# RMSNorm with ReLU: half of VectorE's loop replaced by whole-chunk instructions, with shared reciprocals and the last store split in two

## Chip, cores, metric

One core of one Trainium2 chip. The metric is the device time of one execution in microseconds (us); all times below are of runs with a granted clock of 1.0 in each. The "span" of a profile is some 1.3 us shorter than the time of the same run (158.9 against 160.25 for the profiled run of the kernel before). Times of single DMA packets ("packet records") are given here on the same clock as the instructions of the profile. The recorded prediction and expectations read them from an origin some 0.035 us earlier, so their packet times are that much too high against their issue times (the first packet of the kernel before starts at 1.755 us, and the prediction has 1.79).

## The reference

```python
def reference(x, gamma, eps):          # x: (16, 1024, 512) float32, gamma: ones(512), eps 1e-5
    rms = np.sqrt(np.mean(x ** 2, axis=-1, keepdims=True) + eps)
    x_norm = x / rms * gamma
    return np.maximum(x_norm, 0).astype(np.float32)
```

16,384 rows of 512 floats: 33.55 MB come in and 33.55 MB go out.

## The kernel before

Each of the 128 partitions takes 128 rows, as eight chunks of 16 rows (4 MB over all partitions). The kernel keeps six chunks on chip, so chunks 6 and 7 reuse the places of chunks 0 and 1, once those have been stored. SyncE (SP) issues every large transfer on one queue, in this order: the loads of chunks 0 to 5 (chunk 0 in two halves), the stores of chunks 0 and 1, the loads of chunks 6 and 7, a store of chunks 2 and 3 together (rows 32 to 63, "the middle store" below), a store of chunks 4 and 5, and the stores of chunks 6 and 7. ScalarE squares and sums the rows and takes the roots, 8 rows a pass. VectorE scales, multiplies by gamma and cuts at 0.

```python
    # SP: the order of the transfers, and what each waits for
    order = [(L, 0, G), (L, G, G)] + [(L, i * K, K) for i in range(1, nslots)] + [
        (S, 0, K), (S, K, K), (L, room, K), (L, room + K, K),
        (S, 2 * K, 2 * K), (S, 4 * K, 2 * K), (S, room, K), (S, room + K, K)]
    ...
        if kind == S:
            if order[m - 1][0] == L:                       # the first store after a load
                nc.sync.wait_ge(tick, 6 if a == 0 else 11)
            nc.sync.wait_ge(done, (a + r) // G)
        elif a >= room:
            take(nc.sync, sems[order.index((S, a - room, r))], 16)
        transfer(m)
    ...
    # VectorE: 12 passes of 8 rows for chunks 0 to 5 ...
    ndyn = nslots * per
    with nc.vector.Fori(0, ndyn) as gi:
        ...
        nc.vector.wait_ge(sq, 1)                            # ScalarE's root of this pass
        nc.vector.reciprocal(...)                           # 8 columns
        for j in range(G):                                  # 8 times 512 elements
            r = nc.vector.scalar_tensor_tensor(out=row, in0=row, scalar=rstd[...],
                in1=gamma_sb, op0=ALU.mult, op1=ALU.mult)
            if j == G - 3:
                r.then_inc(tick, 1)
        ...
        nc.vector.tensor_scalar_max(out=blk, in0=blk, scalar1=0.0).then_inc(done, 1)
    # ... and chunks 6 and 7 whole
    for i in range(nslots, nchunks):
        nc.vector.wait_ge(sq, per * (i - nslots + 1))
        nc.vector.reciprocal(...)                           # 16 columns
        nc.vector.tensor_tensor(out=blk, in0=blk, in1=fac[:, :, None].to_broadcast([P, K, d]), op=ALU.mult)
        nc.vector._custom_dve(dve_ops.TENSOR_MUL_SAT, out=blk, in0=blk,      # times gamma, cut at 0
            in1=gamma_sb[:, None, :].to_broadcast([P, K, d]), s0=float("inf"), s1=0.0).then_inc(done, per)
```

## Time and profile before

| | before |
|---|---|
| time, median of 6 runs | 160.28 us (160.15 to 160.50) |
| span of the profiled run | 158.9 us |
| moved by the large queue | 67.11 MB, 98.3% of the 16 DMA engines' span |
| VectorE busy | 129.4 us (81%), last instruction ends at 145.5 |
| ScalarE busy | 86.3 us (54%), last root near 114 |

The groups of instructions of the page, with busy us and mean ns of one, and after the second bar the idle time in front of them:

```profile
L153 DVE SCALAR_TENSOR_TENSOR slots<-slots,rstd,gamma_sb 128x512 f32 x96 | 64.7, 746 | 1.8 <-DVE rstd L148 1.8
L160 DVE TENSOR_SCALAR slots<-slots x12 | 27.5, 2294 | 0.4
L173 DVE CUSTOM_DVE_ANT_1 slots<-slots,gamma_sb 128x8192 f32<-128x8192 f32 x2 | 17.4, 8693 | 0.3
L170 DVE TENSOR_TENSOR slots<-slots,rstd 128x8192 f32<-128x8192 f32 x2 | 17.4, 8692 | 0.1
```

### The profile page before, as it was taken

The page shows a single profiled execution, that of the slowest core. Times are in us where ns is not written, and L with a number is a line of the kernel's source. Part 1 is how long each engine was busy: PE and PEld are TensorE (multiplying, and loading weights), DVE is VectorE, ACT ScalarE, POOL GpSimd, SP SyncE. Part 2 cuts the span into 40 slices and gives each one's busy share as a digit, 9 for nine tenths or more (in the row PEclk, how much of TensorE's full clock was granted, in tenths as well). Part 3 has the DMA queues.
Part 4 walks back from the last instruction along what each step waited for, and adds up shares of the span by engine and source line. Part 5 has one row for each costly group of instructions (what it writes and reads, how often), then busy time and mean ns, then how long its engine had stood idle before and what let it go on. Part 6 is the DMA issues. An engine that isn't in the chain of part 4 may idle for free.

```text
span 158.9 us, 902 instructions
## 1 busy us (share of the span) xinstructions
DVE 129.4 (81%) x128; ACT 86.3 (54%) x273; POOL 0.8 (0%) x6
## 2 busy tenths in 40 slices
DVE  0013999999999999999999999999999999996000
ACT  0388919889889989988930098898600000000000
POOL 1000000000000000000000000000000000000000
DMA  6999999999999999999999999996997998999996
GB/s 194 406 454 449 470 404 396 495 429 396 429 487 404 396 462 462 396 404 495 421 396 404 503 412 396 528 495 297 528 478 313 528 412 379 396 396 503 412 404 264
DMA packets 2168, 67.12 MB, mean 422 GB/s; under 512 B 244, under 2 KB 244, under 8 KB 248
## 3 DMA queue, kind: packets, MB, share of 16 engines
q1 hardware_dynamic: 2160, 67.11, 98.3%
q10 hardware_dynamic: 8, 0.01, 0.0%
HBM read 33.56 MB, written 33.55 MB: 422 GB/s over the span
## 4 chain that ended last, share of the span: by engine, by line
DVE 51%; issue 18%; DVEq 5%; ACT 3%; ACTq 0%; POOLq 0%
DVE slots L153 27%; DVE slots L170 11%; DVE slots L173 11%; DVEq L153 3%; ACT junk L130 3%; DVE rstd L148 1%; DVEq L143 1%; DVEq L148 0%; ACTq L130 0%; DVE rstd L168 0%; DVE slots L160 0%; ACT rms L135 0%; DVEq L162 0%; DVEq L172 0%; ACTq L135 0%
## 5 line engine op out<-in xcount | busy, mean ns | idle before, releaser
L130 ACT ACTIVATE junk<-slots 128x512 f32 x128 | 74.4, 581 | 21.9 <-POOLq L117 17.4
L153 DVE SCALAR_TENSOR_TENSOR slots<-slots,rstd,gamma_sb 128x512 f32 x96 | 64.7, 746 | 1.8 <-DVE rstd L148 1.8
L160 DVE TENSOR_SCALAR slots<-slots x12 | 27.5, 2294 | 0.4
L130 ACT ACTIVATION_READ_ACCUMULATOR junk<-slots x128 | 23.9, 186 | 0.0
L173 DVE CUSTOM_DVE_ANT_1 slots<-slots,gamma_sb 128x8192 f32<-128x8192 f32 x2 | 17.4, 8693 | 0.3
L170 DVE TENSOR_TENSOR slots<-slots,rstd 128x8192 f32<-128x8192 f32 x2 | 17.4, 8692 | 0.1
L148 DVE RECIPROCAL rstd<-rms x12 | 2.3, 195 | 5.4 <-ACT rms L135 5.4
L141 DVE LOAD_MASK_SELECT gamma_sb<-gseed x1 | 0.0, 14 | 8.0 <-DMA gseed<-in_gamma_dram 8.0
L135 ACT ACTIVATE rms<-ss,eps_sb x16 | 4.8, 301 | 1.8
L123 ACT ACT_TABLE_LOAD x1 | 1.3, 1283 | 4.0 <-issue 4.0
L141 DVE STREAM_SHUFFLE gamma_sb<-gseed 128x512 f32<-128x512 f32 x1 | 0.7, 717 | 0.0
L112 POOL MEMSET gseed<- 128x512 f32 x1 | 0.5, 525 | 1.9 <-POOLq L97 1.9
L168 DVE RECIPROCAL rstd<-rms 128x16 f32<-128x16 f32 x2 | 0.5, 246 | 0.0
L203 POOL MEMSET const-bfloat16-1.0<- 128x1 bf16 x1 | 0.1, 101 | 0.0
L203 POOL MEMSET const-uint8-127<- 128x1 uint8 x1 | 0.1, 101 | 0.0
L203 POOL MEMSET const-float32-0.0<- 128x1 f32 x1 | 0.1, 98 | 0.2 <-issue 0.2
L203 POOL MEMSET const-float32-1.0<- 128x1 f32 x1 | 0.1, 98 | 0.0
L113 POOL MEMSET eps_sb<- 128x1 f32 x1 | 0.1, 98 | 0.0
## 6 DMA issues: line engine op xcount, KB each, us to landing
slots<-in_x_dram SPq DMA_DIRECT2D x7, 4096.0 KB, 29.8
out_dram<-slots SPq DMA_DIRECT2D x4, 4096.0 KB, 17.4
slots<-in_x_dram SPq DMA_DIRECT2D x2, 2048.0 KB, 9.7
out_dram<-slots SPq DMA_DIRECT2D x2, 25.6
gseed<-in_gamma_dram ACTq DMA_DIRECT2D x1, 8.0 KB
```

Source lines behind the costliest of these rows:

```text
L112: nc.gpsimd.memset(gseed, 0.0).then_inc(sem_z, 1)
L123: nc.scalar.preload_act_table(ACTF.Sqrt)
L130: a = nc.scalar.activation(out=junk[:, j, :], in_=slots[:, bass.ds(base + j * d, d)], func=ACTF.Square, accum_out=ss[:, bass.ds(col + j, 1)])
L135: nc.scalar.activation(out=rms[:, bass.ds(col, G)], in_=ss[:, bass.ds(col, G)], func=ACTF.Sqrt, bias=eps_sb, scale=inv_d).then_inc(sq, 1)
L141: nc.vector.stream_shuffle(gamma_sb, gseed, [0] * 32)
L143: with nc.vector.Fori(0, ndyn) as gi:
L148: nc.vector.reciprocal(out=rstd[:, bass.ds(col, G)], in_=rms[:, bass.ds(col, G)]).then_inc(sv, 1)
L153: r = nc.vector.scalar_tensor_tensor(out=row, in0=row, scalar=rstd[:, bass.ds(col + j, 1)], in1=gamma_sb, op0=ALU.mult, op1=ALU.mult)
L160: nc.vector.tensor_scalar_max(out=blk, in0=blk, scalar1=0.0).then_inc(done, 1)
L168: nc.vector.reciprocal(out=fac, in_=rms[:, i * K:(i + 1) * K]).then_inc(sv, 1)
L170: nc.vector.tensor_tensor(out=blk, in0=blk, in1=fac[:, :, None].to_broadcast([P, K, d]), op=ALU.mult).then_inc(sv, 1)
L173: nc.vector._custom_dve(dve_ops.TENSOR_MUL_SAT, out=blk, in0=blk, in1=gamma_sb[:, None, :].to_broadcast([P, K, d]), s0=float("inf"), s1=0. ...
```

## The change

The intent: VectorE issues fewer, larger instructions. It loops over chunks 0 to 2 only and takes chunks 3 to 7 whole; chunks 4 and 5 share one reciprocal, and so do chunks 6 and 7. The middle store is held until 10 groups of 8 rows are done (it waited for the eleventh pass's tick), and the last chunk's second multiply and its store are cut into two halves of 8 rows.

```diff
+    looped = 3
...
-        (S, 2 * K, 2 * K), (S, 4 * K, 2 * K), (S, room, K), (S, room + K, K)]
+        (S, 2 * K, 2 * K), (S, 4 * K, 2 * K), (S, room, K),
+        (S, room + K, G), (S, room + K + G, G)]
...
-                nc.sync.wait_ge(tick, 6 if a == 0 else 11)
+                nc.sync.wait_ge(*((tick, 6) if a == 0 else (done, 10)))
...
-    ndyn = nslots * per
+    ndyn = looped * per
...                                  (the loop over chunks 6 and 7 is replaced by)
+    for first, last in ((3, 3), (4, 5), (6, 7)):
+        nc.vector.wait_ge(sq, per * (last + 1 - looped))
+        whole(nc.vector.reciprocal, out=rstd[:, first * K:(last + 1) * K],
+              in_=rms[:, first * K:(last + 1) * K])
+        nc.vector.wait_ge(sv, steps)
+        for i in range(first, last + 1):
+            blk = here(i * K, K)
+            whole(nc.vector.tensor_tensor, out=blk, in0=blk,
+                  in1=rstd[:, i * K:(i + 1) * K, None].to_broadcast([P, K, d]), op=ALU.mult)
+            nc.vector.wait_ge(sv, steps)
+            r = G if i == nchunks - 1 else K
+            for a in range(i * K, (i + 1) * K, r):
+                blk = here(a, r)
+                nc.vector._custom_dve(dve_ops.TENSOR_MUL_SAT, out=blk, in0=blk,
+                    in1=gamma_sb[:, None, :].to_broadcast([P, r, d]),
+                    s0=float("inf"), s1=0.0).then_inc(done, r // G)
```

`whole` emits an instruction, increments the semaphore `sv` on its end and counts.

## The prediction

> **What bounds the kernel now.** I read the page's summary first, to ask which resource is never idle.
>
> ```profile
> span 158.9 us, 902 instructions
> DVE 129.4 (81%) x128; ACT 86.3 (54%) x273; POOL 0.8 (0%) x6
> DMA  6999999999999999999999999996997998999996
> q1 hardware_dynamic: 2160, 67.11, 98.3%
> HBM read 33.56 MB, written 33.55 MB: 422 GB/s over the span
> ```
>
> VectorE (DVE) is busy 81% of the span and is the largest part of the "chain that ended last", which invites the reading "VectorE bounds it". But the one queue that carries x in and the result out occupies the 16 DMA engines for 98.3% of the span. The dips in the DMA row are a binning effect: in the records of single DMA packets, cut across slices of 2 us, the share is 1.00 in every slice from 2.5 us to the last one. A 32,768 B packet takes 1213 ns, a 65,536 B one 2419 and a 16,384 B one 611, so 27.0 GB/s per engine whatever the piece, 432 GB/s together. 67.11 MB at 432 GB/s is 155.3 us. Add 1.79 us before the first packet and about 0.5 us from the last packet to the last signal, and some 1.3 us is left of 158.9: the ramp of the first packets, and the lag of the slowest engine, whose last packet ends at 158.46 while the others end between 157.63 and 158.13. So this is a DMA-bound kernel with a full pipe, and the question for any VectorE change is only whether a transfer is ever issued too late.
>
> For that I read the timeline of the issuing engine (SP) and of VectorE.
>
> ```profile
> 58.55 0.82 SPq L82 DMA_DIRECT2D out_dram<-slots  x2
> 71.38 10.26 SPq L82 DMA_DIRECT2D slots<-in_x_dram  x2
> 98.45 0.34 SPq L82 DMA_DIRECT2D out_dram<-slots  x1
> 110.08 0.34 SPq L82 DMA_DIRECT2D out_dram<-slots  x1
> 127.81 0.33 SPq L82 DMA_DIRECT2D out_dram<-slots  x1
> 145.53 0.33 SPq L82 DMA_DIRECT2D out_dram<-slots  x1
> ```
>
> Columns: start, duration, place. Against these the packet records give the times at which the transfers in front leave the engines: the store of rows 32 to 63, issued at 98.45, sends its first packets at 99.54 to 100.13, engine by engine[...]. The store issued at 110.08 waits in the queue until about 119, the one of 127.81 until 138.3, and the last, of 145.53, starts at 147.96 to 148.77. All wait behind another transfer; the slack of the 98.45 store is by far the smallest.
>
> [...]the first load is issued at 0.73 us, its first packets start on the 16 engines at 1.79 to 2.24. I use the measured 1.06 to 1.51 us. [...]the 4096-element tensor_scalar of L160 takes 2294 ns, the 8192-element tensor_tensor of L170 8692. [...]
>
> **The change part by part.**
>
> ```profile
> 59.88 2.29 DVE L160 TENSOR_SCALAR slots<-slots  x1
> 62.09 0.19 DVE L148 RECIPROCAL rstd<-rms  x1
> 80.48 0.30 ACT L135 ACTIVATE rms<-ss,eps_sb  x1
> 109.97 0.25 DVE L168 RECIPROCAL rstd<-rms 128x16 f32<-128x16 f32 x1
> 110.25 8.69 DVE L170 TENSOR_TENSOR slots<-slots,rstd 128x8192 f32<-128x8192 f32 x1
> 119.09 8.69 DVE L173 CUSTOM_DVE_ANT_1 slots<-slots,gamma_sb 128x8192 f32<-128x8192 f32 x1
> 127.70 0.25 DVE L168 RECIPROCAL rstd<-rms 128x16 f32<-128x16 f32 x1
> ```
>
> *Removed:* six of twelve loop passes. A pass starts every 7.98 us, so 16 rows cost 15.96 us. *Added:* three chunks of 16 rows taken whole. Start to start a whole chunk is 127.70 - 109.97 = 17.73 us: 0.28 for the reciprocal, 8.84 for the multiply with its wait, 8.61 for the custom one. So whole chunks are dearer, 1.77 us each, since they lose the double-rate maximum. Over the whole, VectorE's instruction count falls but its work grows.
>
> Walking VectorE's new order, with those intervals: the loop's sixth pass ends as now, and chunk 3 starts at 62.09. Its custom instruction starts at 62.09 + 0.28 + 8.84 = 71.21, and the next instruction could start at 79.82. That is the shared reciprocal of chunks 4 and 5, which needs ScalarE's twelfth root: 80.48 + 0.30 = 80.78, and 0.16 us to release VectorE (first one: root ends at 14.05, reciprocal starts at 14.21), so 80.94. This is a **new wait of 1.1 us**. A 32-column reciprocal I put at 0.35 us (8 columns 195 ns, 16 columns 246, so 6.4 ns a column). Multiply at 81.33, custom at 90.17, its end at 98.86.
>
> There `done` reaches 10, which the store of rows 32 to 63 now waits for: issue at 98.86 + 0.03 = **98.89 in place of 98.45**. Going on: chunk 5's multiply 98.78, custom 107.62 to 116.31, store of rows 64 to 95 issued 116.34 (now 110.08; needed by about 119). Shared reciprocal of chunks 6 and 7 at 116.23; ScalarE ends its sixteenth root near 114, so no wait. Multiply 116.62, custom 125.46 to 134.15, store of chunk 6 issued 134.18 (now 127.81; needed at 138.3 less 1.5). Chunk 7: multiply 134.07, first half 142.91 to 147.34, store issued **147.37**; second half 147.26 to 151.69, store issued **151.72**. VectorE thus ends 6.2 us later than its 145.5 of now.
>
> What that does to the DMA. Middle store: descriptors ready at 98.89 + 1.06 to 1.51, which is 99.95 to 100.40, on engines that become free at 99.54 to 100.13. The engines idle 0.3 to 0.4 us on average, for the first time. But the end is set by the slowest engine, free at 100.13: it loses 0 to 0.27, say 0.15, plus something for a first packet after idleness (the first load's first packets took 719 to 1502 ns against 611; behind a store I put 0.15 to 0.3). First half-store: ready at 148.43 to 148.88, against engines free at 147.96 to 148.77 plus about 0.35 of delay: some engines lose 0.1 more. Second half-store: ready at 152.78 to 153.23, its predecessor runs 8 x 0.611 = 4.89 us from 148.4 on, so until at least 153.2: no loss. Packets of 16 KB: 16 x 611 = 9.78 us against 8 x 1.213 = 9.70, so 0.07. Sum: 0.15 + 0.2 + 0.05 + 0.07, about 0.45 us later.
>
> The split of the last store is what pays for VectorE's lateness. Unsplit, the last store would be issued at about 151.6 (134.07 + 8.84 + 8.69), ready at 152.7 or later, and need 9.7 us more: past 162.4, or some 4 us too late.
>
> The metric's run is 160.31 where the span is 158.9 (a constant near 1.4). So 160.31 + 0.45 = **160.75 us**.
>
> **The rivals.** (a) *The DMA queue hides everything:* [...]only the 0.07 of smaller packets is seen: 160.3 to 160.4. For it: the store is now issued 1.09 us ahead of its first packet[...]. Against it: those 1.09 are just the shortest latency that the first load shows, so there may be no slack left. (b) *VectorE becomes the bound at the end:* if each whole chunk costs 0.3 us more than the two seen, or the shared reciprocals wait longer, then the last halves are issued 1.5 us later and the last store starts late on idle engines: 151.72 + 1.5 + 1.5 + 4.9 + 0.5 = 160.1 of span, 161.5 of time. For it: no run shows a whole chunk beside loads and a busy ScalarE throughout. Against: chunk 6 ran beside ScalarE till 114 and took the same 8.69 as chunk 7. (c) *VectorE was the bound and fewer instructions help:* the chain of waits speaks for it, since it runs along VectorE to 145.5. The packet records refute it, as the last store waits another 2.4 us for the engines; and whole chunks cost more, not less. I give it no time below 160.
>
> **Range and chances.** Rival (a) gives the low edge, 160.2 with the runs' scatter of 0.1; the sum with all its terms at their larger values (0.27 + 0.5 + 0.2 + 0.07) gives 161.3, and (b) 161.5. Range 160.2 to 161.4. Faster by 2% would mean 157.1, less than the DMA work plus its ends allow: 0.01. Slower by 2%, 163.5, needs VectorE's last half 3 us behind my sum: 0.02. Within 2%: 0.97.
>
> **What would show each step right or wrong.** Two reciprocals of 32 columns, the first waiting about 1.1 us for ScalarE; five pairs of 8.69 us[...]; VectorE ending near 151.7; stores issued at 98.9, 116.3, 134.2, 147.4 and 151.7; in the packet records a first gap on the engines near 100 us, and perhaps one near 148.4, and none elsewhere. A DMA share of 1.00 through 100 us makes (a) right. An idle pipe between the last two stores makes (b) right. The prediction is wrong if the packets' own durations change, which nothing here would explain.

The sum came to 0.45 us over 160.31, so 160.75. What the traces change for the reader:

- The 432 GB/s are measured (32,768 B in 1213 ns on each of 16 engines, in the profiles before and after alike). That no faster rate is to be had is not shown; the prediction takes the measured rate as given.
- The 4.43 us of each half in VectorE's walk: half of the whole one's 8692 ns would be 4.35 us, which puts the last two issues 0.08 and 0.17 us earlier. The 0.05 us for the first half-store are reckoned with the 4.43. 4.42 us was measured.
- "Descriptors ready", and in late8's expectation "reach an idle engine", stands for the issue plus a measured delay to the first packet: here that of the first load (1.06 to 1.51 us on 15 engines, 1.91 on the last, on the prediction's clock). The profile shows issues and packets only.
- In the packet records of the kernel before, the middle store's first packet follows the end of the engine's last load by 2 to 3 ns on 15 engines, and one engine is idle for 0.12 us, from 99.70.
- The "double-rate maximum" is, in the trace, the loop's tensor_scalar: 2294 ns for 4096 elements, 0.56 ns an element, against 1.06 for the custom multiply (8693 ns for 8192).

## The result

Ratios in this document are the mean time of one kernel's fast runs over that of the other's of the same rounds, so they are not quite the ratio of the medians quoted.

| | before | after |
|---|---|---|
| time, median | 160.28 us (6 runs, 160.15 to 160.50) | 160.11 us (6 runs, 159.92 to 160.22) |
| ratio | | 0.9986, 95% interval 0.9973 to 0.9999 |
| VectorE's last instruction ends | 145.5 us | 151.1 us |

Within 2%, as expected, but on the other side of 160.28 from the predicted 160.75, and under the range's low edge of 160.2. The summary of the page after:

```profile
span 158.6 us, 770 instructions
DVE 135.2 (85%) x76; ACT 86.3 (54%) x273; POOL 0.8 (0%) x6
DMA  6999999999999999999999999997969969999997
q1 hardware_dynamic: 2304, 67.11, 98.6%
```

VectorE is busy 5.8 us longer with 52 fewer instructions, and the large queue still fills the DMA engines. VectorE's timeline after (start, duration, idle time in front in brackets) and the timeline of SP's issues:

```profile
59.70 2.29 DVE L161 TENSOR_SCALAR slots<-slots  x1
61.91 0.24 DVE L168 RECIPROCAL rstd<-rms 128x16 f32<-128x16 f32 x1
71.03 8.69 DVE L185 CUSTOM_DVE_ANT_1 slots<-slots,gamma_sb 128x8192 f32<-128x8192 f32 x1
80.61 0.35 DVE L168 RECIPROCAL rstd<-rms 128x32 f32<-128x32 f32 x1 [0.89 <-ACT rms L136]
89.82 8.69 DVE L185 CUSTOM_DVE_ANT_1 slots<-slots,gamma_sb 128x8192 f32<-128x8192 f32 x1
...
142.38 8.76 DVE L185 CUSTOM_DVE_ANT_1 slots<-slots,gamma_sb 128x4096 f32<-128x4096 f32 x2
```

```profile
98.54 0.34 SPq L83 DMA_DIRECT2D out_dram<-slots  x1
115.96 0.34 SPq L83 DMA_DIRECT2D out_dram<-slots  x1
133.78 0.33 SPq L83 DMA_DIRECT2D out_dram<-slots  x1
146.84 4.67 SPq L83 DMA_DIRECT2D out_dram<-slots  x2
```

The reader should see that the order is as worked out, down to the new wait of 0.89 us for ScalarE, but all of it 0.2 to 0.6 us ahead of the worked-out times. In the packet records of this profile one engine out of 16 pauses at 99.51 us, for 0.09 us; apart from such pauses near 7 us, where gamma comes in, there is no other of that length.

### The profile page after: what moved, and what is told of

Read it like the earlier page. It is cut to its first block, busy times and chain, and to the rows that moved or that the text cites. A ratio compares the mean times of both kernels' runs of the same rounds, so it can differ in the third digit from the quotient of the medians.

```text
span 158.6 us, 770 instructions
## 1 busy us (share of the span) xinstructions
DVE 135.2 (85%) x76; ACT 86.3 (54%) x273; POOL 0.8 (0%) x6
## 3 DMA queue, kind: packets, MB, share of 16 engines
q1 hardware_dynamic: 2304, 67.11, 98.6%
## 4 chain that ended last, share of the span: by engine, by line
DVE 44%; ACT 27%; issue 6%; ACTq 4%; DVEq 0%; POOLq 0%
ACT junk L131 26%; DVE slots L185 22%; DVE slots L168 22%; ACTq L131 3%; ACTq L126 1%; DVE rstd L168 0%; ACT rms L136 0%; ACTq L136 0%; ACTq L139 0%; DVEq L181 0%; POOLq L118 0%
## 5 line engine op out<-in xcount | busy, mean ns | idle before, releaser
L185 DVE CUSTOM_DVE_ANT_1 slots<-slots,gamma_sb 128x8192 f32<-128x8192 f32 (+1 forms) x6 | 43.5, 7269 | 0.6
L168 DVE TENSOR_TENSOR slots<-slots,rstd 128x8192 f32<-128x8192 f32 x5 | 43.4, 8689 | 0.1
L154 DVE SCALAR_TENSOR_TENSOR slots<-slots,rstd,gamma_sb 128x512 f32 x48 | 32.3, 747 | 0.9 <-DVE rstd L149 0.9
L161 DVE TENSOR_SCALAR slots<-slots x6 | 13.8, 2294 | 0.2
L149 DVE RECIPROCAL rstd<-rms x6 | 1.2, 196 | 5.1 <-ACT rms L136 5.1
L168 DVE RECIPROCAL rstd<-rms 128x32 f32<-128x32 f32 (+1 forms) x3 | 0.9, 315 | 0.9 <-ACT rms L136 0.9
```

The lines of the kernel that those rows point to most:

```text
L149: nc.vector.reciprocal(out=rstd[:, bass.ds(col, G)], in_=rms[:, bass.ds(col, G)]).then_inc(sv, 1)
L168: emit(**kw).then_inc(sv, 1)
```

## The experiments

**A substitution first.** The custom operation TENSOR_MUL_SAT could not be run in new kernels here, so every experiment has this in its place (gamma is 1, so the result is the same). It is called "the substitution" below, and the first two runs are its controls.

```diff
-nc.vector._custom_dve(dve_ops.TENSOR_MUL_SAT, out=blk, in0=blk, in1=gamma..., s0=float("inf"), s1=0.0)
+nc.vector.scalar_tensor_tensor(out=blk, in0=blk, scalar=0.0, in1=gamma..., op0=ALU.max, op1=ALU.mult)
```

**after_sub: the changed kernel with the substitution alone.**

> The changed kernel with the custom multiply replaced by a scalar_tensor_tensor that takes the maximum with 0 and multiplies by gamma (same result here, since gamma is 1; the custom operation could not be run again). Control for the runs that follow. Theory (the DMA queue is the bound, any VectorE time that meets the store deadlines is hidden): 8.7 us for 16 rows again, stores issued within 0.3 us of 98.5, 116.0, 133.8, 146.8 and 151.2, time 160.0 to 160.3, ratio to the kernel before 0.998 to 1.001. Rival (the shorter instruction stream itself gave the 0.14%): ratio 0.9986 again with an interval that excludes 1.

Measured: 160.27 us (160.17 to 160.31, 5 runs), ratio to the kernel before 0.9991 (0.9978 to 1.0005). By shape, the control's instructions and those of the changed kernel agree to 2 ns:

```profile
L185 DVE SCALAR_TENSOR_TENSOR slots<-slots,gamma_sb 128x8192 f32<-128x8192 f32 x4 | 34.8, 8694 | 0.4
L185 DVE SCALAR_TENSOR_TENSOR slots<-slots,gamma_sb 128x4096 f32<-128x4096 f32 x2 | 8.8, 4422 | 0.0
```

```profile
L185 DVE CUSTOM_DVE_ANT_1 slots<-slots,gamma_sb 128x8192 f32<-128x8192 f32 x4 | 34.8, 8692 | 0.5
L185 DVE CUSTOM_DVE_ANT_1 slots<-slots,gamma_sb 128x4096 f32<-128x4096 f32 x2 | 8.8, 4423 | 0.0
```

The first fence is the control, the second the changed kernel. The control stands for it. Its interval holds both 1 and 0.9986, so this run does not decide on the rival.

**before_sub: the kernel before with the substitution alone.**

> The kernel before with only that same substitution in its two whole chunks. Should be the kernel before in all else: ratio 1.000 within 0.1%, stores issued at 98.4, 110.1, 127.8, 145.5. If it is 0.9986 or below, the substitution itself matters and the control above has to be read with it.

Measured: 160.37 us (160.30 to 160.45), ratio 1.0000 (0.9987 to 1.0014), stores issued at 98.42, 110.05, 127.75 and 145.44. The substitution is neutral.

**split_only: the kernel before with only the split of the last store.**

```diff
-        (S, 2 * K, 2 * K), (S, 4 * K, 2 * K), (S, room, K), (S, room + K, K)]
+        (S, 2 * K, 2 * K), (S, 4 * K, 2 * K), (S, room, K),
+        (S, room + K, G), (S, room + K + G, G)]
```

> The kernel before (with the substitution) with only the last 16 rows leaving in two stores of 8; both halves are issued together near 145.5, ahead of need. Theory (packets of 16 KB cost 611 ns against 1213 for 32 KB, so 0.07 us more for the last store, and the slowest engine's lag varies from run to run): ratio 1.0000 to 1.0010. Rival (the smaller packets shorten the tail, and that is where the changed kernel's 0.17 us came from): ratio 0.998 to 0.999.

Measured: 160.52 us (160.45 to 160.70), ratio 1.0014 (1.0000 to 1.0028). That is 0.15 us over before_sub's median, twice the 0.07 us reckoned from the packets' durations; the interval of the ratio is wide enough for both. The rival falls: the split by itself gains nothing, and it is not where the 0.17 us comes from.

**no_split: the changed kernel with its last chunk whole.**

```diff
-        (S, room + K, G), (S, room + K + G, G)]
+        (S, room + K, K)]
...
-            r = G if i == nchunks - 1 else K
+            r = K
```

> The changed kernel (with the substitution) with its last 16 rows in one multiply and one store. The store is then issued near 151.2, its packets start 1.06 to 1.5 us later on engines idle since 148 to 148.8, and need 9.7 us: span about 162.5, time about 163.9, 3.7 us or 2.3% over the changed kernel. Rival (VectorE's lateness was never near a deadline, so the split pays nothing): 160.1.

Measured: 163.72 us (163.53 to 163.88, 4 runs), ratio 1.0213 (1.0197 to 1.0228), 3.45 us over the control's median. The issue of the last store, from SP's timeline:

```profile
151.06 0.33 SPq L83 DMA_DIRECT2D out_dram<-slots  x1
```

In the packet records the 16 engines fall idle between 147.92 and 148.65, and each stays so for 3.2 to 4.1 us, until this store's packets start at 151.89 to 152.04, which is 0.83 to 0.97 us after the issue. The cost is 0.25 us under the 3.7 expected, as that start came earlier than the 1.06 to 1.5 us allowed for. So VectorE does pass a deadline when it is late, and the split is what keeps it inside.

**late8, late16, late32: how late may the middle store be?** SP does N pairs of increments just ahead of this store, N = 8, 16, 32. Nothing else moves.

```diff
             nc.sync.wait_ge(done, (a + r) // G)
+            if a == 2 * K:
+                for _ in range(N):
+                    nc.sync.sem_inc(pad, 1)
+                    nc.sync.sem_inc(pad, -1)
```

> The substituted changed kernel, with 8 pairs of +1 and -1 on a spare semaphore put on the issuing engine just ahead of the store of rows 32 to 63, so that this store is issued later (I do not know yet by how much; the trace will say) and nothing else moves. Theory (descriptors reach an idle engine about 0.9 to 1.1 us after the issue, as the runs so far bound it): each engine idles by issue + 1.0 minus the time it becomes free (99.6 to 100.2), the slowest engine last; with an issue at t the time is 160.27 + max(0, t + 1.0 - 100.2). At 99.1 that is 160.27, though the mean engine idles 0.2 to 0.3. Rival of my prediction (1.06 to 1.51 us and an extra 0.15 to 0.3 for a first packet after idleness): at 99.1 it would be 160.7 or more.

> The same with 16 pairs. Theory: 160.27 + max(0, t + 1.0 - 100.2) for the issue time t in the trace; at t = 99.6 that is 160.65. Prediction's figures: 161.1 or more at t = 99.6. Rival (the queue hides it): 160.27.

> The same with 32 pairs. Theory: 160.27 + max(0, t + 1.0 - 100.2); at t = 100.8 that is 161.9, with all 16 engines idle by about 1.2 to 2.1 us near 100 and the engines started again within some 0.3 us of each other, so that their lags against each other are evened out. Rival (later stores have enough slack to make the loss good): 160.3.

The issues from SP's timelines, late8, late16 and late32 in this order:

```profile
99.49 0.34 SPq L84 DMA_DIRECT2D out_dram<-slots  x1
```

```profile
100.56 0.34 SPq L84 DMA_DIRECT2D out_dram<-slots  x1
```

```profile
102.75 0.34 SPq L84 DMA_DIRECT2D out_dram<-slots  x1
```

| | issue | first packets on the 16 engines | after the issue | idle of an engine, least to most | time (5 runs) | theory |
|---|---|---|---|---|---|---|
| after_sub | 98.79 | 99.65 to 100.14 | behind the load | 0.17 in all, on one to three engines | 160.27 | |
| late8 | 99.49 | 100.32 to 100.48 | 0.84 to 0.99 | 0.29 to 0.93 | 160.59 (160.51 to 160.70) | 160.27 + 0.29 = 160.56 |
| late16 | 100.56 | 101.40 to 101.55 | 0.84 to 0.99 | 1.41 to 1.92 | 161.61 (161.49 to 161.70) | 160.27 + 1.36 = 161.63 |
| late32 | 102.75 | 103.59 to 103.74 | 0.84 to 0.99 | 3.66 to 4.25 | 163.80 (163.75 to 163.87) | 160.27 + 3.55 = 163.82 |

The theory column is the formula with the issue time put in. It holds to 0.03 us, which is partly luck: its 160.27 is from another chip (6, the late runs are from 11), on which the kernel before took 160.38 us against 160.28 here. Taken by the ratios to the kernel before, each of the three lost 0.11 to 0.17 us more than the formula says. The slope does not depend on this: from late8 to late32 the issue moves by 3.27 us and the time by 3.21. So every microsecond that the middle store is late beyond about 99.2 (99.1 by the ratios) is paid nearly in full, and nothing later makes it good. Two figures of my prediction are replaced by measured ones: an idle engine gets its first packet 0.84 to 0.99 us after the issue in these three runs, not 1.06 to 1.51, and that packet takes 2.45 to 2.47 us against 2.42 of the others, so 0.03 to 0.05 us more, not 0.15 to 0.3. The restart spreads over 0.15 us, where 0.3 was expected, and the idle times expected for late32 (1.2 to 2.1) were written for an issue at 100.8; each pair turned out to be 0.12 to 0.13 us. One more thing to see: after such a restart the engines end within 0.2 us of each other (late8: 158.62 to 158.80), where in the kernel before the last one is 0.7 us behind the middle one.

**no_hold: the middle store issued as soon as its rows are done.**

```diff
-                nc.sync.wait_ge(*((tick, 6) if a == 0 else (done, 10)))
+                nc.sync.wait_ge(*((tick, 6) if a == 0 else (done, 8)))
```

> The substituted changed kernel with the store of rows 32 to 63 held only until its own rows are done (8 groups, near 79.7 us), not until 10. Its issue then follows the last load's, near 81.7 us, 18 us ahead of need. Theory (the hold costs at most the 0.1 to 0.2 us gap on one early engine, which is not the slowest): no gap near 100 us, ratio to the kernel before 0.998 to 1.000, the same as the control's 0.9991 within 0.1%. Rival (the hold keeps the store from running beside the loads and pays): slower by 0.3% or more.

Measured: 160.26 us with a wide scatter (159.98 to 160.84, 6 runs), ratio 1.0004 (0.9989 to 1.0019).

```profile
81.84 0.38 SPq L83 DMA_DIRECT2D out_dram<-slots  x1
```

Issued 18 us ahead of need, the store leaves no gap near 100. Neither side comes out clean: the time is not slower by 0.3%, but one run of six is (160.84), and the ratio is 0.13% above the control's, where 0.1% was the limit set. In the profiled run, a fast one, packets near 98.5 us took up to 0.6 us longer than usual, where the store's first packets meet the last loads. Whether that makes the slow runs is taken up by unshared_late9, without success.

**no_mult: VectorE relieved of 17.4 us.** The multiply by the reciprocal is left out for chunks 6 and 7. The result is wrong; it still passed the comparison, presumably since each row's rms is near 1.

```diff
+            if i < 6:
                 whole(nc.vector.tensor_tensor, ...)
                 nc.vector.wait_ge(sv, steps)
```

> The substituted changed kernel without the multiply by the reciprocal in its last two chunks (wrong result on purpose). VectorE ends near 134 in place of 151.5, and its busy time falls by 17.4 us. Theory (DMA queue and its slowest engine are the bound): the last stores are only issued earlier, near 125.3, 129.7 and 134.0, and the time stays: 160.1 to 160.4. Rival (VectorE is part of the bound): lower by more than 0.5 us.

Measured: 160.16 us (160.00 to 160.31), ratio 0.9994 (0.9981 to 1.0007). VectorE's timeline, then SP's:

```profile
116.22 17.36 DVE L186 SCALAR_TENSOR_TENSOR slots<-slots,gamma_sb 128x8192 f32<-128x8192 f32 x3
```

```profile
124.94 9.00 SPq L83 DMA_DIRECT2D out_dram<-slots  x3
```

The last three stores are issued from 124.9 to 133.6, the last of them 17.8 us earlier than the control's, and the time stays. VectorE is not the bound of the changed kernel.

**unshared: one reciprocal for each whole chunk.**

```diff
-    for first, last in ((3, 3), (4, 5), (6, 7)):
+    for first, last in ((3, 3), (4, 4), (5, 5), (6, 6), (7, 7)):
```

> The substituted changed kernel with one reciprocal for each of the five chunks in place of the shared ones: the wait for ScalarE's twelfth root (0.9 us in the control) goes, chunk 4 starts at once near 79.6, the store of rows 32 to 63 is issued about 0.9 us earlier (98.5 - 0.9 = 97.7) and VectorE ends some 0.5 us earlier. Theory: hidden, ratio to the kernel before 0.998 to 1.000, no gaps near 100 us. Rival (the shared reciprocals' wait costs time): 0.3 us or more faster than the control's 160.27.

Measured: 160.32 us (160.03 to 160.80, 6 runs), ratio 1.0005 (0.9990 to 1.0020). The wait for ScalarE is gone and the middle store is issued at 97.33 in place of 98.79:

```profile
97.33 0.34 SPq L83 DMA_DIRECT2D out_dram<-slots  x1
```

The median does not follow, so the wait that the sharing brings is hidden. The scatter is that of no_hold.

**after_act_wide and before_act_wide: is ScalarE's instruction stream what slows the last engine?** The packet records raised this. In most runs one DMA engine ends later than the rest (in the kernel before at 158.42 us, the others at 157.60 to 158.10), and packets of one engine take longer than the others' while stores run in 60 to 78 us. I call the sum over packets of "its duration less the usual one" the excess. On the last engine of the kernel before it is 0.38 us in 60 to 78 us, where no other has over 0.01, then 0.30 in 98 to 118 us and 0.06 after that. The edit (wrong results):

```diff
-        for j in range(G):
+        for j in range(1):
             a = nc.scalar.activation(
-                out=junk[:, j, :], in_=slots[:, bass.ds(base + j * d, d)], ...)
+                out=junk[...8 rows...], in_=slots[:, bass.ds(base, G * d)], ...)
```

> The substituted changed kernel with ScalarE's eight 512-element squares a group made one instruction over 4096 elements (wrong result on purpose), so that ScalarE runs an eighth of its large instructions. In the packet records of all runs so far the engine that ends last carries an excess of packet time in 60 to 78 us and in 98 to 118 us and none after 118, where ScalarE has stopped. If ScalarE's many instructions cause it, the excess in both windows falls to below 0.1 us and the time by 0.1 to 0.4 us, to about 160.0. If VectorE's loop causes it, the excess of 98 to 118 stays at 0.2 and the time at 160.2 to 160.3.

> The same alteration in the substituted kernel before. If ScalarE's instructions cause the slow engine's excess: below 0.1 us in both windows and the time 160.0, equal to the changed kernel with the same alteration. If VectorE's loop of small instructions causes it: the excess stays near 0.4 and 0.3 us, and the time near 160.37; then the changed kernel, with half the loop, is faster by 0.1 us for that reason. If both do, something between, with the changed kernel ahead by about 0.1 us.

Measured: 160.49 us (160.44 to 160.51), ratio 1.0016 (1.0003 to 1.0029), and 160.34 us (160.28 to 160.69), ratio 1.0011 (0.9998 to 1.0024). Neither is faster. By their times they are inconclusive: ScalarE's first root comes earlier, the first two stores are issued at 57.5 and 57.3 (58.6 and 58.5 in after_sub and before_sub) beside loads that last until 61, and the records show new excess there, up to 0.9 and 1.1 us on an engine in 6 to 60 us. The alteration moved what it was meant to leave alone. The excess in 62 to 78 us, where stores alone run, does tell something: it is 0.01 us in after_act_wide and 0.06 in before_act_wide, against 0.25 and 0.38 in after_sub and before_sub. So ScalarE's narrow squares, or the time that it is busy (8.0 us of these 16, in place of 14.6), are needed for nearly all of it; VectorE's loop makes a difference of 0.06 beside wide squares and of 0.13 beside narrow ones (one profile each of the wide ones).

**looped4: is it VectorE's loop?** One chunk more in the loop; it fills 62 to 78 us, and from 80.6 us on VectorE goes as in the control.

```diff
-    looped = 3
+    looped = 4
-    for first, last in ((3, 3), (4, 5), (6, 7)):
+    for first, last in ((4, 5), (6, 7)):
```

> The control with four chunks in the loop in place of three; its loop runs to 78.0 us, then VectorE waits for ScalarE's twelfth root as the control does, so from 80.6 us on both run alike. Theory (the small looped instructions of VectorE slow one DMA engine while stores run): excess in 60 to 78 us back to 0.38, time 0.1 to 0.2 us over the control on the same chip. Rival (the 0.1 us between the kernels has another cause, the later half of VectorE's order or the split store, or is chance): excess as the control's and the same time within 0.06 us.

It ran on one chip with both controls:

> The control again, for comparison on the same chip: ratio to the kernel before 0.9985 to 0.9995; excess of the slow engine in 60 to 78 us 0.16 to 0.27.

> The substituted kernel before again: ratio 1.000, excess of the slow engine in 60 to 78 us 0.38.

VectorE's timeline in looped4, then in after_sub2:

```profile
75.86 2.29 DVE L161 TENSOR_SCALAR slots<-slots  x1
80.67 0.35 DVE L168 RECIPROCAL rstd<-rms 128x32 f32<-128x32 f32 x1 [2.52 <-ACT rms L136]
81.06 8.69 DVE L168 TENSOR_TENSOR slots<-slots,rstd 128x8192 f32<-128x8192 f32 x1
```

```profile
71.42 8.69 DVE L185 SCALAR_TENSOR_TENSOR slots<-slots,gamma_sb 128x8192 f32<-128x8192 f32 x1
80.85 0.35 DVE L168 RECIPROCAL rstd<-rms 128x32 f32<-128x32 f32 x1 [0.74 <-ACT rms L136]
81.24 8.69 DVE L168 TENSOR_TENSOR slots<-slots,rstd 128x8192 f32<-128x8192 f32 x1
```

Both wait for the same root and go on alike. The times, and the excess of all data packets that start in 62 to 78 us (in the window of the expectation, 60 to 78, it is 0.43, 0.42 and 0.32 for the first three):

| run | VectorE in 62 to 78 us | excess, us | time, us |
|---|---|---|---|
| before_sub2 | loop | 0.37 | 160.37 (160.13 to 160.69), ratio 1.0003 |
| looped4 | loop | 0.37 | 160.40 (160.27 to 160.57), ratio 1.0002 |
| after_sub2 | whole | 0.24 | 160.21 (160.09 to 160.49), ratio 0.9994 |
| before, before_sub, split_only | loop | 0.34, 0.38, 0.36 | |
| after, after_sub, no_split, no_hold, unshared, no_mult, late8, late16, late32, unshared_late9 | whole | 0.21 to 0.25 | |

The excess came back to that of the kernel before; it is 0.34 to 0.38 in all five profiles with the loop there, and 0.21 to 0.25 in all others of the same ScalarE. That part is shown: beside ScalarE's narrow squares, VectorE's loop in this stretch costs DMA packets 0.13 us. How the one acts on the other is not shown. Followed from packet to packet, one engine carries nearly all of the excess (0.34 of 0.37 in before_sub2), and in the profiles of before and before_sub2 it is the engine that ends last (158.42 and 158.53). In the profile of the changed kernel two engines carry it, and both end 0.3 to 0.4 us ahead of the last, at 158.09. The time followed by 0.19 us between the medians, in the direction and size expected, but single runs overlap (five against five), so that these 0.13 us are what the kernel gained is likely and not proved.

**unshared_late9: does the early middle store make the scatter?** The edit is unshared's, with 9 pairs of increments ahead of the middle store as above.

> The kernel with five separate reciprocals, with the store of rows 32 to 63 delayed by 9 pairs on a spare semaphore (0.13 us each by the traces, so issued at 98.5 in place of 97.3). Theory (a store issued well ahead of the last load's end runs beside loads and makes single engines lose up to 0.5 us, in some runs): all runs within 160.0 to 160.4, no run near 160.8. Rival (the scatter of up to 160.8 comes from the separate reciprocals or is chance): one run in three or so above 160.5 again.

Measured: 160.17 us (160.08 to 160.58, 5 runs), ratio 0.9997 (0.9983 to 1.0011), middle store issued at 98.61. One run of five lies above 160.5, which is between what the two theories say, and before_sub2, where no store is early, had one of 160.69 in the same rounds. Left open.

None of the versions beats the changed kernel clear of the noise. The engines move 432 GB/s by their packets' durations and are busy for 98.6% of the changed kernel's span, and no_mult found nothing to win on VectorE; what is left at that rate lies in the start of the first packets (1.74 us in the changed kernel) and the lag of the last engine (0.30 us behind the middle one).

## Why the prediction was right or wrong

**Right: the bound.** The DMA engines set the time. no_mult takes 17.4 us off VectorE and wins nothing that the noise would not cover, and VectorE's 5.6 us of later end cost nothing.

**Right: the cost of the parts and VectorE's order.** Five pairs of 8.69 us; a new wait for ScalarE of 0.89 us (1.1 predicted); a 32-column reciprocal of 351 ns (350 predicted); halves of 4423 ns (4.43 us in the walk). The order ran ahead of mine by 0.18 us at 61.91, since in that run ScalarE's first root came earlier (it ended at 13.86 against 14.05), and by 0.35 us at the middle store (98.54 against 98.89): the release after ScalarE's root took 0.03 us (80.58 to 80.61) where 0.16 was assumed, and the steps from there to the issue 17.93 us against 17.95.

**Right: the split pays for VectorE's lateness.** "Some 4 us too late" without it; no_split measured 3.45 us.

**Wrong: the term for the middle store,** "it loses 0 to 0.27, say 0.15, plus something for a first packet after idleness ... I put 0.15 to 0.3", with another 0.05 for the first half-store: 0.40 of the 0.45 us. It measured nothing. The mechanism is real, as the three late runs show, but its latency was mis-sized. I took 1.06 to 1.51 us from the first load of the kernel (1.02 to 1.47 on the right clock, on 15 of the 16 engines); in mid-kernel it was 0.84 to 0.99 in the three late runs, and a first packet after idleness took 0.03 to 0.05 us more, not 0.15 to 0.3. With that, even my 98.89 gives first packets from 99.73 to 99.88 on, ahead of the slowest engine's 100.10. One early engine idles for 0.09 us (0.12 in the kernel before) and hands on nothing, since it is not the last to end. These two engines got their first packet 1.06 and 1.37 us after the issue, so 0.84 to 0.99 does not hold for every engine. No gap of the engines appears at the first half-store. So rival (a) was right in its outcome, though the slack is no more than some 0.3 to 0.7 us and its 160.3 to 160.4 was also too high. Without this term the prediction would have been 160.35; the 0.24 us from there to 160.11 are another matter, the next points.

**Mis-sized: the smaller packets.** 0.07 us predicted; split_only has 0.15 us over its control, with a scatter that allows for either.

**Missing: a gain.** I had allowed for no effect of VectorE's instructions on the DMA packets, and named a change of the packets' own durations as a sign that the prediction is wrong. That sign came. looped4 puts it at 0.13 us of packet time for the loop in 62 to 78 us, which about offsets the split. What remains of the measured 0.17 us (0.11 and 0.12 between the medians of the two controls and the kernel before) is of the size of the scatter between runs; the sum 0.15 - 0.13 does not reach it, and I leave that rest open. The two profiles show where it lies, not why: the middle one of the 16 engines ends 0.09 us later than before, and the last one 0.32 us earlier.

**The range** was too narrow at the low edge because it was built from 160.2 as a floor, three runs' scatter around the old time, although nothing said that the time could not fall by 0.1 us.

**Slips in the working** that change no reading: the four terms sum to 0.47 and not 0.45; by the figures given the engines would have idled 0.44 us on average, not 0.3 to 0.4; and the profiled run is 160.25, so that the constant between time and span is 1.3 and not 1.4.

## What to carry to other kernels

When one queue fills the DMA engines from end to end, ask of each store how long ahead of need it is issued, on the engine that ends last: here VectorE could end 5.6 us later for free, as every store met its deadline, while past the middle store's deadline a further 3.27 us of delay cost 3.21 (late8 to late32). Take the latency for that sum from the middle of the kernel, by delaying one issue on purpose (0.84 to 0.99 us here), and not from its first transfer (1.02 to 1.47). And if VectorE is late at the very end, halving the last piece of work and its store can save a few microseconds (3.45 here) at a small cost (0.07 reckoned, 0.15 measured).
